# Leading weight tiles of a diffusion backbone: the first norm split into scale, rstd and shift

## The chip, the cores and the metric

One core of a Trainium2 chip runs the whole program. The metric is the device time of one execution in microseconds (us), the median of several runs. TensorE is called PE, VectorE DVE, ScalarE ACT, GpSimd POOL, and SyncE SP; SP here only issues transfers.

## The reference

Two layers over 256 latent tokens and 256 context tokens, 1024 wide, float32. Each layer is half a SwiGLU feed-forward, a token mixer (latent attention in layer 0, windowed attention in layer 1), and another half feed-forward. Before each of the six sub-layers stands a norm with adaLN. What the change touches is the first of them, in layer 0:

```python
mx = split(silu(c) @ mod_w[0] + mod_b[0], 9)       # shift, scale, gate, ...; the same for c_ctx
h  = rms_norm(x, g) * (1 + scale) + shift
x  = x + 0.5 * gate * ((silu(h @ w_gate) * (h @ w_up)) @ w_out)
```

In the kernel's words: x stands transposed, 8 tiles of 128 features by 512 tokens (both streams side by side). With G = g (1 + scale) per feature and r = rstd per token, h = x G r + shift, and a product with a weight tile W is W·h.

## The kernel before, in words

Float32 products are made of three passes: each operand is split into a high and a low half (the cast on ACT, line 198, the difference on DVE, line 199), and `mm3` multiplies high by high, high by low and low by high (lines 226, 227, 228). A weight tile of 128 outputs has 8 k-blocks, so 24 such matmuls of 512 columns; 44 tiles make the gate and up halves of a feed-forward. Split weights lie in rings of four (`whi`, `wlo`), raw weights in a ring of three, PE's results in eight banks.

The opening of the program, before the first feed-forward, is what the change rewrites. SP issues the loads in program order: the four loads of x (512 KB each), then for each k the four pieces of adaLN column k (shift and scale, two halves of the contraction each, 256 KB), with the four leading weight tiles (512 KB, into the `big` ring) behind columns 0, 1, 3 and 5. Eight transfers are in flight at a time: a load waits for the eighth before it. ACT loads four small constants on its own queue.

`fill(40)` keeps PE busy with multiplies of ones that nobody reads (line 88). ACT squares x (line 964), DVE adds the squares, PE sums them over the features and turns the root's inverse back over the tokens (lines 972 to 989): r is in SBUF before the first product. For each k, `mod_sums` multiplies the columns by silu(c) (16 small matmuls, line 143), ACT copies the sums, PE transposes them (line 151), DVE adds bias and halves and makes the gain (lines 158 to 160). `inputs(k)` makes h of tile k: DVE x G r (line 999), ACT adds the shift and casts (line 1001), DVE takes the low half (line 1002). `lead_products` then multiplies tile k with as many of the four leading weight tiles as are split. All four are held in banks until `ffn` asks for them.

The order on each engine is a static list that a scheduler writes when the program is built: an engine works its list from front to back and waits at an instruction whose operands are missing. `behind(ins)` pins a place in it.

From the third f on `ffn` calls `pump`, which advances the adaLN of later sub-layers in the background: DVE multiplies and adds columns (lines 169 and 171), PE sums them (line 177). For each f, ACT takes silu of the gate bank (line 426), DVE multiplies it with the up bank (line 428), and the product is split.

Of the kernel before, what the change touches and what calls it, by code (L numbers as in the profile page):

```python
# [37 lines left out]
def hybrid_backbone_kernel(ctx, tc, t, out):  # L38
# [40 lines left out]
    nc.vector.memset(ones, 1.0)  # L79
# [3 lines left out]
    def fill(n, after=None):  # L83

        b = bank()
        with behind(after):
            for _ in range(n):
                nc.tensor.matmul(b[:, :P], lhsT=ones, rhs=ones, start=True, stop=True)

    def behind(ins):  # L90

        return tc.issue_after(ins.ins) if ins else nullcontext()
# [33 lines left out]
            elif c in (2, 8):  # L126
                nc.vector.tensor_scalar_mul(v, v, 0.5)

    def load_column(k):

        raws = [[], []]
        for i in range(2):
            for c in range(2):
                raw = r2k().bitcast(F32)
                nc.sync.dma_start(raw, t["modo"][k, c, i])
                raws[c].append(raw.rearrange("p (k n) -> p k n", k=4))
        return raws

    def mod_sums(raws):
        psA = bank()  # L140
        for kt in range(KT // 2):
            for j in range(4):
                nc.tensor.matmul(psA[32 * j:32 * j + 32, :P], lhsT=cond32[:, j % 2 * 4 + kt, :], rhs=raws[j // 2][j % 2][:, kt],
                                 start=(kt == 0), stop=(kt == KT // 2 - 1), skip_group_check=True)
        return psA

    def mod_on_pe(k, psA, n=0, after=None):
        sA = tmp()[:, :P]
        nc.scalar.copy(sA, psA[:, :P])
        psB = bank()[:, :P]  # L150
        turned = nc.tensor.transpose(psB, sA, ident)
        if n:
            fill(n, turned)
        vB = psB.rearrange("p (c i r) -> p c i r", c=2, i=2)
        v = mod[0][:, :, :2 * KT].rearrange("p s (c k) -> p c s k", c=2)[:, :, :, k]
        bias = modb[:, 0, :2 * KT].rearrange("p (c k) -> p c k", c=2)[:, :, k:k + 1].to_broadcast([P, 2, 2])
        with behind(after):
            nc.vector.tensor_tensor(v, vB[:, :, 0, 0:2], bias, ALU.add)
        nc.vector.tensor_tensor(v, vB[:, :, 1, 0:2], v, ALU.add)
        nc.vector.scalar_tensor_tensor(coefA[0][:, :, 0, k], v[:, 1], 1.0, ng[:, 0, 0, k:k + 1].to_broadcast([P, 2]), ALU.add, ALU.mult)  # L160

    def mod_in_background(l, c, streams):
        acc = [big().bitcast(F32)[:, :1024] for _ in streams]
# [102 lines left out]
    def load_table(func, q):  # L266

        d = small(1)
        nc.scalar.activation(d, q[:, 0:1], func, scale=1.0 if func == AF.Sqrt else -1.0)

    class Sublayer:


        def __init__(self, l, sub, streams, first, leads=None, both=2):
            self.l, self.sub, self.streams, self.first = l, sub, streams, first
            self.leads, self.both = leads or streams, both
            self.squares = {s: Squares(KT) for s in streams}
            self.hs = []
            self.lead, self.r = [], {}
            self.end = None  # L280

        def grown(self, s, d):
            if s in self.streams:
# [128 lines left out]
    def ffn(sl, nxt, per_tile=0, late=0):  # L412
        l, which, streams = sl.l, sl.sub // 2, sl.streams
        w = T * len(streams)
        outs = sl.products(ffn_specs(l, which))
        done = sl.end
        for g, (f0, f1) in enumerate(GROUPS):
            gu = []
            for f in range(f0, f1):
                n = 0 if f < late else per_tile + (6 * late <= f < 8 * late)  # L420
                pump(n // 2, done)
                og = next(outs)
                pump(n - n // 2, done)
                ou = next(outs)
                sg = tmp()
                nc.scalar.activation(sg[:, :w], og[:, :w], AF.Silu)  # L426
                pr = tmp()
                nc.vector.tensor_tensor(pr[:, :w], ou[:, :w], sg[:, :w], ALU.mult)  # L428
# [529 lines left out]
        return s  # L958

    sl = Sublayer(0, 0, (0, 1), ffn_specs(0, 0)[:4])  # L960
    squares = None
    for d in range(KT):
        q = tmp()
        nc.scalar.activation(q, xs[d], AF.Square)
        if squares is None:
            squares = q
        else:
            nc.vector.tensor_tensor(squares, squares, q, ALU.add)
    load_table(AF.Sqrt, q)
    total = bank()  # L970
    for j in range(4):
        nc.tensor.matmul(total[:, j:j + 1], lhsT=squares[:, j * P:(j + 1) * P], rhs=ones[:, 0:1], start=True, stop=True)
    raws, wraws = [], []
    for k in range(KT):
        raws.append(load_column(k))
        if k in (0, 1, 3, 5):
            ap, n = sl.first[len(wraws)]
            wraws.append(weight_raw(ap, n, big().bitcast(F32)))

    sums0 = mod_sums(raws[0])  # L980
    root = small()
    nc.scalar.activation(root, total[:, 0:4], AF.Sqrt, scale=1.0 / D, bias=eps)
    nc.vector.reciprocal(root, root)
    wide = bank()
    for j in range(4):
        nc.tensor.transpose(wide[:, j * P:(j + 1) * P], root[:, j:j + 1].to_broadcast([P, P]), ident)
    rstds = [strip() for _ in range(2)]
    for r, cols in zip(rstds, SL):
        nc.scalar.copy(r, wide[:, cols])
    def lead_weight(after=None):  # L990
        with behind(after):
            wt = weight_split(wraws[len(sl.lead)])
        sl.lead.append((wt, bank(), P))

    lead_weight()
    def inputs(k):
        for s in range(2):
            y = strip()
            nc.vector.scalar_tensor_tensor(y, xs[k][:, SL[s]], sl.gain(s, k), rstds[s], ALU.mult, ALU.mult)
            hi, lo = sl.place(s, k)  # L1000
            sl.hi = nc.scalar.activation(hi, y, AF.Identity, bias=sl.shift(s, k))
            sl.end = nc.vector.scalar_tensor_tensor(lo, y, sl.shift(s, k), hi.bitcast(F32), ALU.add, ALU.subtract)

    done = [0] * 4

    def lead_products(n, k1):

        for k in range(k1):
            for i in range(n):
                if done[i] <= k:  # L1010
                    wt, o, M = sl.lead[i]
                    mm3(o, sl.terms(wt, M, slice(0, TT)), (k,), KT)
        done[:n] = [k1] * n

    mod_on_pe(0, sums0, 3)
    inputs(0)
    for k in range(1, KT + 1):
        if k < KT:
            mod_on_pe(k, mod_sums(raws[k]), 5 if k == 1 else 0, sl.end if k == 1 else None)
        lead_products(len(sl.lead), k)  # L1020
        if k < KT:
            inputs(k)
        if k in (1, 3, 5):
            lead_weight(sl.hi)
    qng = load_const("qng", (P, 4))
    kvng = load_const("kvng", (P, 2))
    ropeC = load_const("ropeC", (P, T))
# [117 lines left out]
```

## Time and profile before

| | |
|---|---|
| median of 3 runs | 1699.57 us (1696.93 to 1700.79) |
| the profiled execution's own time | 1699.09 us |
| its span, first to last instruction | 1697.3 us |
| mean granted PE clock | 0.999 |
| PE busy | 1672.6 us, 99% |
| DVE busy | 1080.8 us, 64% |
| ACT busy | 645.4 us, 38% |
| DMA | 243.75 MB, mean 144 GB/s |

A timeline row reads: start, duration, engine, line, operation, output<-inputs, shapes, count, and in brackets the idle time just before and what ended it. An fp32 matmul of two plain fp32 operands shows as two records, so x32 of line 143 are 16 matmuls. Matmuls overlap: a row of 0.39 us may start 0.23 us after the one before. A row of the windows view reads: stretch, its length, then busy time and count for PE, PEld, DVE, ACT and POOL, then granted clock, DMA share and GB/s; where one engine is asked for, its column alone. A row of the waits view reads: who waited for whom, us in total, times, longest. A row of groups reads: count, busy us, mean ns, idle before; a tile's row has the shortest, median and longest duration in ns and the first and last start.

### The profile page before, as it was taken

The page shows a single profiled execution, that of the slowest core. Times are in us where ns is not written, and L with a number is a line of the kernel's source. Part 1 is how long each engine was busy: PE and PEld are TensorE (multiplying, and loading weights), DVE is VectorE, ACT ScalarE, POOL GpSimd, SP SyncE. Part 2 cuts the span into 40 slices and gives each one's busy share as a digit, 9 for nine tenths or more (in the row PEclk, how much of TensorE's full clock was granted, in tenths as well). Part 3 has the DMA queues.
Part 4 walks back from the last instruction along what each step waited for, and adds up shares of the span by engine and source line. Part 5 has one row for each costly group of instructions (what it writes and reads, how often), then busy time and mean ns, then how long its engine had stood idle before and what let it go on. Part 6 is the DMA issues. An engine that isn't in the chain of part 4 may idle for free.

```text
span 1697.3 us, 23433 instructions
## 1 busy us (share of the span) xinstructions
PE 1672.6 (99%) x9294; PEld 1417.5 (84%) x9294; DVE 1080.8 (64%) x1538; ACT 645.4 (38%) x1132; POOL 222.5 (13%) x186
## 2 busy tenths in 40 slices
PE   9999999999999999999999999999999999999997
PEld 7888878888788898788888897888888898789997
DVE  6776777645668568856847365644433367778886
ACT  4421322235556353222222353222222366654444
POOL 0000000004132130000000130000000253133332
PEclk9999999999999999999999999999999999999999
DMA  9655556531211126644645335735332222155553
GB/s 345 220 164 183 167 186 194 162 124 57 88 50 63 56 84 200 207 149 154 208 144 172 107 112 196 234 123 162 114 100 92 95 88 77 62 161 175 174 186 113
DMA packets 71536, 243.75 MB, mean 144 GB/s; under 512 B 8577, under 2 KB 9345, under 8 KB 71425
## 3 DMA queue, kind: packets, MB, share of 16 engines
q1 hardware_dynamic: 70560, 241.54, 43.7%
q8 instruction: 73, 1.20, 0.3%
q10 hardware_dynamic: 864, 0.70, 0.1%
q14 instruction: 39, 0.31, 0.1%
HBM read 241.16 MB, written 1.05 MB: 143 GB/s over the span
## 4 chain that ended last, share of the span: by engine, by line
PE 79%; DMA 5%; DVE 5%; ACT 4%; POOL 3%; issue 2%; ACTq 0%; DVEq 0%; SPq 0%; POOLq 0%
PE bank L226 25%; PE bank L227 25%; PE bank L228 24%; DMA wraw<-in_woutn 4%; POOL wraw L912 3%; DVE wlo L199 2%; ACT whi L198 2%; DMA r2k<-in_modo 1%; PE bank L177 1%; DVE big L171 1%; PE bank L239 1%; DVE small L454 0%; PE bank L482 0%; PE bank L906 0%; DMA modraw<-in_modw 0%
## 5 line engine op out<-in xcount | busy, mean ns | idle before, releaser
L226 PE MATMUL bank<-r2k,whi 128*128 128x512 f32 (+2 forms) x2434 | 866.7, 357 | 0.9 <-ACT small L918 0.9
L227 PE MATMUL bank<-r2k,whi 128*128 128x512 f32 (+2 forms) x2434 | 861.9, 354 | 2.6 <-DVE r2k L202 1.2
L228 PE MATMUL bank<-r2k,wlo 128*128 128x512 f32 (+2 forms) x2434 | 861.4, 354 | 1.1 <-DVE wlo L199 0.9
L198 ACT CAST whi<-wraw 128x1024 fp32r<-128x1024 f32 (+1 forms) x311 | 319.9, 1033 | 851.1 <-PE bank L227 502.1
L226 PEld LDWEIGHTS bank<-r2k,whi 128*128 128x128 f32 x2434 | 459.1, 189 | 79.5 <-ACT whi L198 9.2
L227 PEld LDWEIGHTS bank<-r2k,whi 128*128 128x128 f32 x2434 | 460.2, 189 | 68.4 <-DVE r2k L202 1.9
L228 PEld LDWEIGHTS bank<-r2k,wlo 128*128 128x128 f32 x2434 | 460.1, 189 | 65.8 <-DVE wlo L199 2.0
L199 DVE TENSOR_TENSOR wlo<-wraw,whi 128x1024 fp32r<-128x1024 f32 (+1 forms) x300 | 363.5, 1218 | 117.2 <-ACT whi L198 110.1
L171 DVE SCALAR_TENSOR_TENSOR big<-modraw,conds,big 128x1024 f32<-128x1024 f32 x189 | 233.3, 1278 | 14.7 <-DMA modraw<-in_modw 14.4
L264 POOL TENSOR_TENSOR strip<-strip 128x256 f32<-128x256 f32 x58 | 57.3, 1002 | 939.5 <-ACT strip L258 465.2
L366 DVE SCALAR_TENSOR_TENSOR x<-bank,mod,x 128x256 f32<-128x256 f32 x168 | 74.3, 478 | 154.0 <-PE bank L228 154.0
L428 DVE TENSOR_TENSOR tmp<-bank,tmp 128x512 f32<-128x512 f32 x66 | 45.6, 690 | 160.7 <-PE bank L228 158.1
L912 POOL TENSOR_TENSOR wraw<-wraw,gate 128x1024 f32<-128x1024 f32 x22 | 63.5, 2888 | 127.2 <-DMA wraw<-in_woutn 127.0
L906 PE MATMUL bank<-whi,r2k 128*128 128x512 f32 x176 | 58.0, 392 | 3.1 <-DVE r2k L927 1.8
L927 DVE TENSOR_TENSOR r2k<-tmp,r2k 128x256 fp32r<-128x256 f32 x22 | 51.0, 2318 | 0.9 <-ACT r2k L926 0.9
L199 DVE TENSOR_TENSOR r2k<-bank,r2k 128x512 fp32r<-128x512 f32 (+2 forms) x73 | 40.7, 593 | 16.1 <-ACT r2k L198 15.6
L199 DVE TENSOR_TENSOR r2k<-tmp,r2k 128x512 fp32r<-128x512 f32 x66 | 45.1, 684 | 1.4 <-ACT r2k L198 1.4
L198 ACT CAST r2k<-tmp 128x512 fp32r<-128x512 f32 x66 | 41.0, 622 | 12.8 <-DVE tmp L428 12.4
L454 DVE TENSOR_REDUCE small<-bank 128x1 f32<-128x512 f32 (+1 forms) x64 | 37.0, 614 | 7.4 <-PE bank L777 7.2
L906 PEld LDWEIGHTS bank<-whi,r2k 128*128 128x128 f32 x176 | 33.0, 188 | 10.2 <-DVE r2k L927 2.2
L426 ACT ACTIVATE tmp<-bank 128x512 f32<-128x512 f32 x66 | 38.9, 590 | 3.7 <-PE bank L228 3.7
L198 ACT CAST r2k<-bank 128x512 fp32r<-128x512 f32 (+2 forms) x73 | 34.4, 524 | 12.7 <-PE bank L228 8.8
(195 smaller groups left out, 1147.5 us busy)
## 6 DMA issues: line engine op xcount, KB each, us to landing
wraw<-in_win SPq DMA_DIRECT2D x172, 512.0 KB, 3.9
modraw<-in_modw SPq DMA_DIRECT2D x128, 512.0 KB, 4.2
wraw<-in_wout SPq DMA_DIRECT2D x48, 448.0 KB, 3.3
wraw<-in_wout SPq DMA_DIRECT2D x24, 512.0 KB, 4.4
wraw<-in_woutn SPq DMA_DIRECT2D x22, 512.0 KB, 3.5
r2k<-in_modo SPq DMA_DIRECT2D x32, 256.0 KB, 6.0
wraw<-in_mwo SPq DMA_DIRECT2D x8, 512.0 KB, 3.5
wraw<-in_swq SPq DMA_DIRECT2D x8, 512.0 KB, 3.5
```

The costliest lines, as they stand in the source:

```text
L171: nc.vector.scalar_tensor_tensor(acc[s], raw, conds[:, kt, s:s + 1], acc[s], ALU.mult, ALU.add)
L198: nc.scalar.copy(hi, src)
L199: return engine.tensor_tensor(lo, src, hi.bitcast(F32), ALU.subtract)
L226: nc.tensor.matmul(o, lhsT=ah, rhs=bh, start=(i == 0), stop=False)
L227: nc.tensor.matmul(o, lhsT=ah, rhs=bl, start=False, stop=False)
L228: nc.tensor.matmul(o, lhsT=al, rhs=bh, start=False, stop=(i == n - 1))
L264: nc.gpsimd.tensor_tensor(self.parts[0], self.parts[0], q, ALU.add)
L366: nc.vector.scalar_tensor_tensor(xs[d][:, SL[s]], o[:, SL[s]], mod[l][:, s, c:c + 1], xs[d][:, SL[s]], ALU.mult, ALU.add)
L428: nc.vector.tensor_tensor(pr[:, :w], ou[:, :w], sg[:, :w], ALU.mult)
L906: nc.tensor.matmul(acc[i][h], lhsT=gu[a][:, rows], rhs=w[b][:, cols], start=(f == 0 and j == 0), stop=(f == NF - 1 and j == 2))
L912: nc.gpsimd.tensor_tensor(raw, raw, gate, ALU.mult)
L927: nc.vector.tensor_tensor(gu[1], u, gu[0].bitcast(F32), ALU.subtract)
```

## The change

W·h is written as r (W·(G x)) + W·shift for the four leading tiles. They multiply z = G x, split into high (ACT, line 1028 of the new file) and low (DVE, line 1029), without r and without the shift. r and the shift join when the banks are read: for the first two f, DVE multiplies the gate and up banks by r, ACT adds the gate's W·shift in the silu, DVE adds the other and multiplies. W·shift comes from 32 small matmuls (line 1110) and a transpose (line 1115), with a table of the shifts in `gate`, a tile that is loaded later on.

The loads are reordered: x 0 and 1, the scale columns of 0 and 1 (four pieces), two weight tiles; then x, the scale columns of two features, and a weight tile, twice; then x 6 and 7 with their scale columns; then all shift columns two features at a time, and two more weight tiles through the `wraw` ring. `mod_sums` now treats two scale or two shift columns in one go, and a product with `both_halves` (line 161) adds the two halves of the contraction where a transpose stood. Squares are taken between the gained tiles, and r after the last of them. The full h is still made (`inputs`, lines 1048 to 1051), for the two further tiles and all others. Twelve fills stand around the first scale sums and twelve around the second.

```diff
-    for d in range(0, KT, 2):
+    def load_x(d):
         nc.sync.dma_start(x_all[:, d:d + 2], t["xT"][:, d:d + 2])
+    load_x(0)
...
+    def mod_sums(raws, n=0):
         psA = bank()
...
         sA = tmp()[:, :P]
         nc.scalar.copy(sA, psA[:, :P])
+        if n:
+            fill(n)
+        v = bank()[:, :4]
+        turned = nc.tensor.matmul(v, lhsT=sA, rhs=both_halves.rearrange("p a s -> p (a s)"), start=True, stop=True)
         if n:
             fill(n, turned)
...
+                if sl.ends is not None and f < 2:
+                    nc.vector.tensor_tensor(sg, og, sl.rstds, ALU.mult)
+                    nc.vector.tensor_tensor(pr, ou, sl.rstds, ALU.mult)
+                    for s in streams:
+                        nc.scalar.activation(sg[:, SL[s]], sg[:, SL[s]], AF.Silu, bias=sl.ends[:, 2 * f, s:s + 1])
+                        nc.vector.scalar_tensor_tensor(pr[:, SL[s]], pr[:, SL[s]], sl.ends[:, 2 * f + 1, s:s + 1], sg[:, SL[s]],
+                                                       ALU.add, ALU.mult)
...
+    scales.append(load_columns(0, 1))
+    load_weight()
+    load_weight()
+    for k in range(2, KT, 2):
+        load_x(k)
+        scales.append(load_columns(k, 1))
+        if k < 6:
+            load_weight()
+    for k in range(0, KT, 2):
+        shifts.append(load_columns(k, 0))
+        if k in (2, 4):
+            more.append(weight_raw(*ffn_specs(0, 0)[len(more) + 4]))
...
+    def gained(d):
+        z = (r2k(), r2k())
+        for s in range(2):
+            nc.scalar.activation(z[0][:, SL[s]], xs[d][:, SL[s]], AF.Identity, scale=sl.gain(s, d))
+            sl.end = nc.vector.scalar_tensor_tensor(z[1][:, SL[s]], xs[d][:, SL[s]], sl.gain(s, d), z[0][:, SL[s]].bitcast(F32),
+                                                    ALU.mult, ALU.subtract)
+        zs.append(z)
...
+    v = mod_sums(scales[0], 6)
+    lead_weight()
+    mod_scale(0, v)
+    gained(0)
+    gained(1)
+    lead_products(1, 1)
+    lead_weight()
+    squares(0)
+    for k in range(2, KT, 2):
+        lead_products(1, k)
+        v = mod_sums(scales[k // 2], 6 if k == 2 else 0)
+        lead_products(len(sl.lead), k)
+        mod_scale(k, v)
+        gained(k)
+        gained(k + 1)
+        if k < 6:
+            lead_weight()
+        q = squares(k)
...
+    lead_products(4, KT - 2)
+    rstds = rstds_of_x()
+    for k in range(0, KT, 2):
+        v = mod_sums(shifts[k // 2])
+        if k == 0:
+            lead_products(4, KT - 1)
+        mod_shift(k, v)
+        inputs(k)
+        inputs(k + 1)
+        if k in (2, 4):
+            more[k // 2 - 1] = (weight_split(more[k // 2 - 1]), bank(), P)
+    lead_products(4, KT)
+    def products_of_inputs():
+        for k in range(KT):
+            for wt, o, M in more:
+                mm3(o, sl.terms(wt, M, slice(0, TT)), (k,), KT)
...
+        for k in range(KT):
+            for j in range(4):
+                nc.tensor.matmul(b[32 * j:32 * j + 32, :P], lhsT=shift32[:, k], rhs=wraws[j][:, k * P:(k + 1) * P],
+                                 start=(k == 0), stop=(k == KT - 1), skip_group_check=True)
```

How the lists of the engines move, at three places. ACT before, from the start to the first operand of a product (`L1001`; `big` holds a raw leading weight tile, `r2k` the operand):

```order
L97 ACTIVATE conds<-c_cond 128x16
L964 ACTIVATE tmp<-x 128x512 x8
L269 ACT_TABLE_LOAD
L269 ACTIVATE small<-tmp 128x1
L982 ACTIVATE small<-bank,eps 128x4
L149 COPY tmp<-bank 128x128
L989 COPY strip<-bank 128x256 x2
L198 CAST whi<-big 128x1024
L149 COPY tmp<-bank 128x128
L1001 ACTIVATE r2k<-strip,mod_127 128x256 x4
```

ACT in the change, to the same point (`L1028`):

```order
L100 ACTIVATE conds<-c_cond 128x16
L216 CAST whi<-big 128x1024 x2
L157 COPY tmp<-bank 128x128
L1012 ACTIVATE tmp<-x 128x512 x2
L216 CAST whi<-big 128x1024 x2
L1028 ACTIVATE r2k<-x,coefA_126 128x256 x4
L157 COPY tmp<-bank 128x128
```

One weight cast stood before the first operand; now all four leading tiles are cast before it, and two of the eight squares remain there.

PE before, from the first fills behind column sums on:

```order
L88 MATMUL bank<-ones 128x128 x3
L143 MATMUL bank<-r2k,cond_124 32x128 x16
L151 MATMUL bank<-c_ident,tmp 128x128
L88 MATMUL bank<-ones 128x128 x5
L226 MATMUL bank<-r2k,whi 128x512
L227 MATMUL bank<-r2k,whi 128x512
L228 MATMUL bank<-r2k,wlo 128x512
L143 MATMUL bank<-r2k,cond_124 32x128 x16
```

PE in the change, from the first product on:

```order
L244 MATMUL bank<-r2k,whi 128x512
L245 MATMUL bank<-r2k,whi 128x512
L246 MATMUL bank<-r2k,wlo 128x512
L244 MATMUL bank<-r2k,whi 128x512
L245 MATMUL bank<-r2k,whi 128x512
L246 MATMUL bank<-r2k,wlo 128x512
L154 MATMUL bank<-r2k,cond_121 32x128 x16
L91 MATMUL bank<-ones 128x128 x6
L161 MATMUL bank<-both_halves,tmp 128x4
L91 MATMUL bank<-ones 128x128 x6
```

Before, no fill stood behind the first product; now twelve do, and the second group of sums, which stood ahead of all products, stands behind six of them.

The last place is the end of the opening, where the last two shift columns are summed. ACT in the change:

```order
L157 COPY tmp<-bank 128x128
L216 CAST whi<-wraw 128x1024 x2
L1050 ACTIVATE r2k<-strip,mod_124 128x256 x2
L157 COPY tmp<-bank 128x128
L1050 ACTIVATE r2k<-strip,mod_124 128x256 x2
```

and PE between its last two products with `both_halves`, and what follows:

```order
L161 MATMUL bank<-both_halves,tmp 128x4
L154 MATMUL bank<-r2k,cond_121 32x128 x16
L245 MATMUL bank<-r2k,whi 128x512
L246 MATMUL bank<-r2k,wlo 128x512
L161 MATMUL bank<-both_halves,tmp 128x4
L244 MATMUL bank<-r2k,whi 128x512
```

The copy that the second `L161` needs now stands behind two casts of further weight tiles. From the seventh weight tile on the lists of PE are alike but for line numbers.

More of the change, by code (lines that the diff above doesn't have):

```diff
@@ L974, in hybrid_backbone_kernel @@
[L974 to L996, printed above, removed]
-        for s in range(2):
[L998 to L1002, printed above, removed]
+    wraws, scales, shifts, more = [], [], [], []
@@ L1010, in lead_products @@
                 if done[i] <= k:
[L1011 to L1019, printed above, removed]
[L1020 to L1024 removed]
+                    (wh, wl), o, M = sl.lead[i]
@@ new lines, in lead_products, with inputs @@
+                    cols = slice(k * P, (k + 1) * P)
+                    mm3(o, {k: ((wh[:, cols], wl[:, cols]), zs[k])}, (k,), KT)
+        done[:n] = [max(k1, n) for n in done[:n]]
+    def inputs(k):
+        for s in range(2):
+            y = strip()
+            nc.vector.scalar_tensor_tensor(y, xs[k][:, SL[s]], sl.gain(s, k), rstds[:, SL[s]], ALU.mult, ALU.mult)
+            hi, lo = sl.place(s, k)
+            sl.hi = nc.scalar.activation(hi, y, AF.Identity, bias=sl.shift(s, k))
+            sl.end = nc.vector.scalar_tensor_tensor(lo, y, sl.shift(s, k), hi.bitcast(F32), ALU.add, ALU.subtract)
@@ new lines, in rstds_of_x @@
+    def rstds_of_x():
+        for j in range(4):
+            nc.tensor.matmul(total[:, j:j + 1], lhsT=totals[0][:, j * P:(j + 1) * P], rhs=ones[:, 0:1], start=True, stop=True)
+        root = small()
+        nc.scalar.activation(root, total[:, 0:4], AF.Sqrt, scale=1.0 / D, bias=eps)
+        nc.vector.reciprocal(root, root)
+        wide = bank()
+        for j in range(4):
+            nc.tensor.transpose(wide[:, j * P:(j + 1) * P], root[:, j:j + 1].to_broadcast([P, P]), ident)
+        r = r2k().bitcast(F32)
+        nc.scalar.copy(r, wide)
+        return r
```

95 lines of the change are left out of this document (63 added, 32 removed).

## The prediction

> **What bounds the kernel now.** The page first: how busy TensorE (PE) is over the whole span, and what it waits for.
>
> ```profile
> span 1697.3 us, 23433 instructions
> ...
> PE 1672.6 (99%) x9294; PEld 1417.5 (84%) x9294; DVE 1080.8 (64%) x1538; ACT 645.4 (38%) x1132; POOL 222.5 (13%) x186
> ```
>
> Then PE's own waits over the whole span, longest first, of which these are the first, the third and the sixth:
>
> ```profile
> PE bank L803 <- ACT r2k L795: 2.5, 1, 2.5
> ...
> PE bank L906 <- DVE r2k L927: 1.8, 1, 1.8
> ...
> PE bank L143 <- DMA r2k<-in_modo: 1.1, 4, 0.4
> ```
>
> No wait later in the program is longer than 2.5 us, so a microsecond that the opening loses or gains passes to the end nearly whole. Busy is no measure of use there: in the first 40 us PE runs throw-away multiplies (L88) and slow column sums. So I count the opening as a ledger: the time at which PE has finished a known amount of weight products, less that amount at its steady pace. The timeline gives the rows; they are not neighbours.
>
> ```profile
> 1.03 11.58 PE L88 MATMUL bank<-ones 128*128 128x128 f32 x80 [1.03 <-DVE ones L79]
> ...
> 18.06 1.28 PE L88 MATMUL bank<-ones 128*128 128x128 f32 x10
> ...
> 19.10 0.48 PE L226 MATMUL bank<-r2k,whi 128*128 128x512 f32 x1
> ...
> 45.10 1.08 PE L143 MATMUL bank<-r2k,cond 128*32 128x128 f32 x32
> 46.11 0.50 PE L226 MATMUL bank<-r2k,whi 128*128 128x512 f32 x1
> ...
> 53.06 0.40 PE L227 MATMUL bank<-r2k,whi 128*128 128x512 f32 x1
> ...
> 61.92 0.39 PE L227 MATMUL bank<-r2k,whi 128*128 128x512 f32 x1
> ...
> 95.79 1.06 PE L177 MATMUL bank<-big,ones 128*32 128x512 f32 x8
> ```
>
> From 53.06 to 61.92 there are 39 steps (13 triples of lines L226 to L228): 0.227 us each. L177 is a good post: in both programs 12 whole weight tiles of 24 products, 288, stand before it on PE. They cost 288 x 0.227 = 65.4 us, so 95.79 - 65.4 = **30.4 us** went to other things: 19.1 until the first product, and 11.3 after it, of which six groups of column sums at 46.11 - 45.10 = 1.01 are 6.1. In that opening the DMA is the other limit:
>
> ```profile
> 0.00:10.00 10.00, 8.97 (x59) 8.97 (x60) 3.75 (x10) 5.82 (x10) 0.19 (x4) 1.00 0.84 301
> 10.00:20.00 10.00, 9.38 (x122) 8.06 (x120) 6.07 (x16) 4.86 (x11) 0.00 (x0) 1.00 1.01 372
> 20.00:30.00 10.00, 9.13 (x118) 6.26 (x118) 7.41 (x20) 5.29 (x11) 0.00 (x0) 1.00 1.05 392
> ```
>
> The last number is GB/s. The queues are full until 30 us.
>
> **The change part by part. First: when the first product can start.** It needs the scale columns of 0 and 1 and x 0 and 1, which are now early. But the order on ACT, shown above, decides otherwise: the four activations L1028 that make the first operand stand behind the casts of all four leading weight tiles, the fourth included, and that tile is the nineteenth transfer of the SP queue. When does it land? In bytes ahead of it and its own: three x loads and four weight tiles of 512 KB, twelve column pieces of 256 KB, 6656 KB. In the kernel before, column 2 ended the same count at 6144 KB (four x loads, two tiles, twelve pieces), and the last of it was waited for until 21.50:
>
> ```profile
> 21.50 1.06 PE L143 MATMUL bank<-r2k,cond 128*32 128x128 f32 x26 [0.27 <-DMA r2k<-in_modo]
> ...
> r2k<-in_modo SPq DMA_DIRECT2D x32, 256.0 KB, 6.0
> ...
> big<-in_win SPq DMA_DIRECT2D x4, 512.0 KB, 6.0
> ```
>
> 512 KB more is 0.524 MB / 392 GB/s = 1.3 us: 22.8. Lower bound: by 20.0 us 3.01 + 3.72 = 6.73 MB had moved in all, and 6656 KB are 6.82 MB, so not before 20.2 at these rates; upper bound some 23.5. I take 22.8, from the row nearest to it. Then one cast and two halves of the operand:
>
> ```profile
> 15.56 1.06 ACT L198 CAST whi<-big 128x1024 fp32r<-128x1024 f32 x1
> ...
> 16.66 1.23 DVE L199 TENSOR_TENSOR wlo<-big,whi 128x1024 fp32r<-128x1024 f32 x1
> ...
> 17.74 0.91 ACT L1001 ACTIVATE r2k<-strip,mod 128x256 fp32r<-128x256 f32 x2
> ...
> 20.73 0.88 DVE L1002 SCALAR_TENSOR_TENSOR r2k<-strip,mod,r2k 128x256 fp32r<-128x256 f32 x2 [0.18 <-ACT r2k L1001]
> ```
>
> 22.8 + 1.06 + 0.91 and 0.1 for the hand-over: first product at **24.9**, against 19.10. What waits behind that cast is everything: ACT's L1028, DVE's L1029, all of PE.
>
> **Second: PE work that is no product, after that start.** Seven groups of column sums instead of six (a group now holds two scale or two shift columns, so eight groups remain, but only one is ahead of the start): 7 x 1.01 = 7.1. Twelve throw-away multiplies stand between the second group and the products; five took 1.28 (18.06, two records each), 0.25 each: 3.0. The row sums of squares and their turning, hidden before the first product until now, stand in the middle of the products:
>
> ```profile
> 12.45 0.95 PE L972 MATMUL bank<-ones,tmp 128*128 128x1 f32 x8
> ...
> 14.34 0.65 PE L986 MATMUL bank<-c_ident,small 128*128 128x128 f32 x4
> ...
> L151 PE MATMUL bank<-c_ident,tmp 128*128 128x128 f32 x8 | 2.3, 285 | 0.4 <-ACT tmp L149 0.4
> ```
>
> 0.95 + 0.65 = 1.6. Seven products with both_halves (L161) take the place of transposes; they are of the kind of L972, 0.24 each, at least half of that if pipelined: 7 x 0.2 = 1.4. New are 32 small products of the shift (L1110), of the shape of L143's 16: 2.0, and one transpose, 0.1. Sum 7.1 + 3.0 + 1.6 + 1.4 + 2.1 = 15.2. The other side of this work is a multiply by rstd and an add that leave L999 to L1002; those are DVE and ACT work, and no PE time comes back for them. Six instead of four tiles before the steady part is only the order of the same 288.
>
> **Third: waits.** On DVE the low half of the fourth tile (1.23) stands before the first L1029 (0.88), while PE has one product of 0.23 to do: 1.2 with the second operand's share. Five round trips over ACT's copy at 0.1: 0.5. At the last shift columns ACT does two casts and two activations, 2 x 1.06 + 0.91, before the copy that PE needs (the rows above); PE has one group and two products, 1.5, to fill it: 2.0 with the copy of 0.27 and hand-overs. DVE then: eight operations instead of two for the first two f, and the sums of the background chunk before L177:
>
> ```profile
> L171 DVE SCALAR_TENSOR_TENSOR big<-modraw,conds,big x14: 1274/1279/1282, 58.9 to 91.3; 128x1024 f32<-128x1024 f32 x14
> ...
> L169 DVE TENSOR_SCALAR big<-modraw,conds x2: 745/746/746, 57.5 to 58.2; 128x1024 f32<-128x1024 f32 x2
> ...
> L428 DVE TENSOR_TENSOR tmp<-bank,tmp 128x512 f32<-128x512 f32 x66 | 45.6, 690 | 160.7 <-PE bank L228 158.1
> ...
> 52.00:95.00 43.00, 43.00 (x190) 35.40 (x189) 36.50 (x37) 17.23 (x24) 0.00 (x0) 1.00 0.67 217
> ```
>
> Now they end at 91.3 + 1.3 = 92.6, 3.2 ahead of PE: this cover is what the change uses up. Its chunk stands on DVE behind the f 0 and 1. From the end of the first six tiles PE has 2.1 of L1110 and 144 products, 34.8 us, until L195. DVE has in that stretch the chunk (2 x 0.746 + 14 x 1.279 = 19.4), five low halves of weights (6.2), four multiplies by rstd and four adds of half width (4 x 0.69 + 4 x 0.44 = 4.5), and three multiplies and five low halves of results (8 x 0.69 = 5.5): 35.6, and it begins some 0.4 later. 1.2 late, bounds 0 and 2.5. Last, the pace after standing still:
>
> ```profile
> 1.00:6.00 5.00, 4.97 (x23) 1.00 0.85 286
> 6.00:12.60 6.60, 6.60 (x62) 1.00 1.04 386
> ```
>
> These are the throw-away multiplies: 4.6 records per us until 6, 9.4 after, though the granted clock reads 1.00. PE started from rest at half pace for 5 us. In the change PE rests from about 17 to 24.9. If that repeats, 2.5 us go, of which the first operands' waits hide about half: I take 1.2, bounds 0 and 2.5. The Trainium skill, "TensorE: Matmul & The Clock Gate", Part 1, states the rule: the array's clock is halved after an idle window of about 3.4 us and comes back after as much sustained work; by it the sum keeps this term, without it the total is 1.2 us lower. The trace agrees for the start (4.6 against 9.4 records per us); it shows no later rest of that length.
>
> Waits: 1.2 + 0.5 + 2.0 + 1.2 + 1.2 = 6.1. **Sum:** 24.9 + 15.2 + 6.1 = 46.2, against 30.4: 15.8 us more. The profiled execution took 1699.1 (span 1697.3), the median is 1699.57: 1699.1 + 15.8 = **1714.9**.
>
> **Edits that I cost at nothing.** The shift columns land late but 4 x 24 products of 0.227 (21.8 us) cover them from 24.9 on: the last piece ends 13312 KB of loads, 7.34 MB past column 2's 6144 KB, so it lands near 21.5 + 7.34 / 0.392 = 40.2, when by my sums less than half of these 96 products are done. Without that cover each pair of columns, 1024 KB, is 2.7 us. The load of gate now waits for L1110; the weight loads behind it wait for their own buffers as long.
>
> **Rivals.**
> (a) The fourth tile is not what decides: it lands as early as the operands could use it. Then the fills end at 12.6 (1.03 + 11.58), one group 1.0, copy, L161 and the scale about 1, the operand 0.9: first product at 15.5. The last scale piece, 8192 KB in, lands at 21.5 + 2.10 / 0.392 = 26.9, early enough behind 72 products. With 15.2 and 3 of the waits (0.5, 2.0, 0.5): 33.7, so 1702.4. For it: no byte of the first operand is missing. Against it: the byte count, 20.2 at the least.
> (b) Faster: halving the column bytes ahead of the products starts PE early and keeps it fed. With no wait at all after the start the ledger is T + 15.2, and it beats 30.4 only for a first product before 15.2; a gain of 0.2% (3.4 us) needs 11.8, and the fills alone hold PE until 12.6. With (a)'s start of 15.5 and all 3.0 of fills inside gaps: 27.7, 1696.4; the groups too would have to fall into gaps for more. For it: the first operand needs half the column bytes. Against it: ACT's order, and 9 us of new or uncovered PE work.
> (c) The loss is given back: a later stage waits now for data that comes at its own time, so that the delay drains away, 1699. Against it: the list of PE's waits has no such entry above 2.5 us.
> (d) DVE becomes the bound in the first feed-forward and holds PE at each chunk: 3 us more, 1718. For it: 36.50 busy of 43; against it: it recovers 3.2 per chunk now.
>
> **How the numbers follow.** Forecast 0.80; (a) 0.08; (b) 0.04; (c) 0.03; (d) 0.05. The forecast's own range: 2.6 off for the earliest landing, 1.2 each for DVE and pace, 1 for fills that run inside a wait, not all together: 1710; upward 1.3 each for DVE and pace, 0.7 for the landing and 1 for buffer waits not counted: 1719. The range 1706 to 1719 leaves out (a), (b), (c) and a little of (d), under 2 in 10. 0.2%, 3.4 us, is about what a measurement of this kernel can tell from no change. Faster: (b), 0.04. Same: (c) and (a) where it stays under 1703, 0.08. Slower: the rest, 0.88.
>
> **What would show it.** First product L244 near 24.9, with the fourth whi cast near 22.8 just before L1028 on ACT; PE idle or at rest from 17 to there; L195 at about 111.6 instead of 95.79, after the same 288 products; no DMA wait on shift columns; the rest of the program shifted as a whole. A first product before 20, or an L195 before 100, would prove me wrong; a later stage shorter than before, too.

## The result, and the profile after

The changed kernel takes **1714.46 us** (median of 4 runs, 1711.34 to 1716.31) against 1698.25 before (4 runs beside it, 1696.7 to 1700.79): ratio **1.009**, 95% interval 1.0072 to 1.0109, slower. Its profiled execution took 1714.77 us, its span is 1713.0.

The page's first rows of the changed kernel:

```profile
span 1713.0 us, 23677 instructions
...
PE 1679.0 (98%) x9399; PEld 1423.9 (83%) x9399; DVE 1082.0 (63%) x1553; ACT 652.5 (38%) x1150; POOL 219.5 (13%) x186
```

PE is busy 6.4 us more, and the span is 15.7 us longer; the other 9.3 are idle time. PE's waits, longest first:

```profile
PE bank L244 <- ACT r2k L1028: 9.7, 1, 9.7
PE bank L830 <- ACT r2k L822: 2.5, 1, 2.5
PE bank L933 <- DVE r2k L954: 1.8, 1, 1.8
```

The second and third are the two longest single waits of the kernel before, unchanged. The first is new: PE stands for 9.7 us ahead of its first product. The timeline over that time, of ACT and of the DVE operation that finishes the first gain:

```profile
16.17 0.17 DVE L174 TENSOR_TENSOR coefA<-coefA,ng 128x4 f32<-128x4 f32 x1
...
18.67 1.04 ACT L216 CAST whi<-big 128x1024 fp32r<-128x1024 f32 x1 [3.34 <-DMA big<-in_win]
...
23.95 1.04 ACT L216 CAST whi<-big 128x1024 fp32r<-128x1024 f32 x1 [4.24 <-DMA big<-in_win]
24.90 1.70 ACT L1028 ACTIVATE r2k<-x,coefA 128x256 fp32r<-128x256 f32 x4
```

The gain is there at 16.34. ACT waits 3.34 us for the third weight tile and 4.24 for the fourth, and only then makes the first operand. Now PE's timeline: the first products, the first two groups of column sums after them, and L195, the post behind the same 288 weight products:

```profile
25.86 0.80 PE L244 MATMUL bank<-r2k,whi 128*128 128x512 f32 x1 [9.69 <-ACT r2k L1028]
27.10 0.79 PE L245 MATMUL bank<-r2k,whi 128*128 128x512 f32 x1 [0.45 <-DVE r2k L1029]
...
29.53 1.94 PE L154 MATMUL bank<-r2k,cond 128*32 128x128 f32 x32
...
37.41 1.08 PE L154 MATMUL bank<-r2k,cond 128*32 128x128 f32 x32
...
65.72 0.38 PE L161 MATMUL bank<-both_halves,tmp 128*128 128x4 f32 x2 [0.79 <-ACT tmp L157]
...
111.93 1.06 PE L195 MATMUL bank<-big,ones 128*32 128x512 f32 x8
```

The post stood at 95.79 and stands at 111.93, 16.1 later; the span is 15.7 longer. The group of sums at 29.53 takes 1.94, the one at 37.41 1.08. The windows view of PE (its busy time, then granted clock, DMA share, GB/s) shows why:

```profile
20.00:21.00 1.00, 0.00 (x0) 1.00 1.03 403
21.00:22.00 1.00, 0.00 (x0) 0.75 1.04 408
22.00:23.00 1.00, 0.00 (x0) 0.50 1.01 391
...
30.00:31.00 1.00, 1.00 (x24) 0.50 1.03 383
31.00:32.00 1.00, 1.00 (x16) 0.63 1.04 373
32.00:33.00 1.00, 1.00 (x12) 1.00 1.02 336
```

During the wait the granted clock falls to 0.50, and it is whole again only near 31.7 (the mean of 0.63 from 31 to 32 puts the step there), 5.9 us after the first product.

### The profile page after: what moved, and what is told of

It is laid out like the page before. It is cut to its first block, busy times and chain, and to the rows that moved or that the text cites. A ratio compares the mean times of both kernels' runs of the same rounds, so it can differ in the third digit from the quotient of the medians.

```text
span 1713.0 us, 23677 instructions
## 1 busy us (share of the span) xinstructions
PE 1679.0 (98%) x9399; PEld 1423.9 (83%) x9399; DVE 1082.0 (63%) x1553; ACT 652.5 (38%) x1150; POOL 219.5 (13%) x186
## 4 chain that ended last, share of the span: by engine, by line
PE 79%; DMA 6%; DVE 5%; ACT 4%; POOL 3%; issue 2%; ACTq 0%; SPq 0%; DVEq 0%; POOLq 0%
PE bank L244 25%; PE bank L245 24%; PE bank L246 24%; DMA wraw<-in_woutn 4%; POOL wraw L939 3%; DVE wlo L217 2%; ACT whi L216 2%; PE bank L195 1%; DMA modraw<-in_modw 1%; DVE small L481 0%; PE bank L509 0%; PE bank L257 0%; PE bank L933 0%; DMA r2k<-in_modo 0%; DVE big L189 0%
## 5 line engine op out<-in xcount | busy, mean ns | idle before, releaser
L217 DVE TENSOR_TENSOR r2k<-bank,r2k 128x512 fp32r<-128x512 f32 (+2 forms) x73 | 40.7, 593 | 16.1 <-ACT r2k L216 15.6
L954 DVE TENSOR_TENSOR r2k<-tmp,r2k 128x256 fp32r<-128x256 f32 x22 | 46.6, 2120 | 0.9 <-ACT r2k L953 0.9
```

The source lines that it names most:

```text
L217: return engine.tensor_tensor(lo, src, hi.bitcast(F32), ALU.subtract)
L954: nc.vector.tensor_tensor(gu[1], u, gu[0].bitcast(F32), ALU.subtract)
```

## The experiments

**One yardstick.** Between the first product and the post, each PE row's step (from its start to the next row's start, its idle time apart) is put to its line; of products only what goes beyond 0.227 us each counts. This table is worked out in that way from the timelines. It sums to the ledger, and each kernel has 288 products in it:

| us | before | after | e3 | e1 | e2 | e4 | e7 |
|---|---|---|---|---|---|---|---|
| first product | 19.10 | 25.86 | 25.82 | 16.39 | 16.95 | 13.59 | 17.70 |
| column sums | 7.58 | 7.93 | 7.07 | 7.07 | 7.79 | 8.88 | 7.21 |
| fills | 0 | 2.92 | 2.78 | 2.78 | 0 | 0 | 0 |
| turning the sums (L151, L161) | 0.14 | 1.34 | 1.35 | 1.33 | 1.38 | 1.36 | 0.64 |
| sums of squares and their turning | 0 | 1.35 | 1.35 | 1.36 | 1.35 | 1.36 | 1.37 |
| the shift's product (L1110, L1115) | 0 | 1.91 | 1.92 | 1.91 | 1.91 | 1.92 | 1.91 |
| idle | 0.88 | 1.24 | 1.53 | 0.79 | 1.18 | 2.28 | 0.85 |
| products beyond 0.227 | 2.71 | 4.00 | 2.70 | 2.72 | 3.16 | 3.54 | 2.79 |
| **ledger** | **30.4** | **46.5** | **44.5** | **34.3** | **33.7** | **32.9** | **32.5** |

**e1_pin: is it the fourth tile's cast?**

```diff
+    first = (sl.hi, sl.end)
...
-            lead_weight()
+            lead_weight(first if k == 2 else (sl.hi, sl.end))
```

`sl.hi` and `sl.end` are the last operations of an operand on ACT and DVE; `lead_weight(after)` pins the cast and the low half behind them; `first` is taken behind the operands of 0 and 1.

> The change with one thing altered: the casts of the third and fourth leading weight tile are pinned on ACT and DVE behind the operands they stood in front of. My theory (ACT's list holds the first operand until the fourth tile lands): first product near 17.4 us instead of 25.9, PE never rests long enough for its clock to fall, background sums L195 near 101 us instead of 111.9, time 1703 to 1705. Rival (the DMA is the limit in the opening, so an earlier start only waits later for scale columns): the start moves but L195 stays above 108, time 1710 or more. Second rival (the start is worth its 8.5 us but the clock's 2 us stay): L195 near 103, 1706.

Measured: 1704.76 us (6 runs, 1703.96 to 1706.69) beside 1699.51, ratio 1.0032 (1.0021 to 1.0044). ACT and PE in its timeline:

```profile
15.43 1.71 ACT L1029 ACTIVATE r2k<-x,coefA 128x256 fp32r<-128x256 f32 x4 [1.03 <-DVE coefA L174]
17.88 1.05 ACT L216 CAST whi<-big 128x1024 fp32r<-128x1024 f32 x1 [0.74 <-DMA big<-in_win]
...
16.39 0.50 PE L244 MATMUL bank<-r2k,whi 128*128 128x512 f32 x1 [0.56 <-ACT r2k L1029]
...
99.73 1.06 PE L195 MATMUL bank<-big,ones 128*32 128x512 f32 x8
```

The operand is made before the third tile is even there, the first product comes 9.5 us earlier and the post 12.2, at 99.73 where some 101 was expected. PE's list is the same in both. At the post, three quarters of the loss were the place of two casts on ACT, with their low halves on DVE; between the medians it is 9.7 of 16.2 us. The loads and their order are unchanged, so these 12.2 were no limit of the DMA alone.

**e3_keepwarm: what is the fallen clock worth?**

```diff
+    fill(36)
```

These are throw-away multiplies between the first column sums and the first product.

> The change with 36 more throw-away multiplies between the first scale sums and the first product, so that PE doesn't rest from 16.2 to 25.9; order otherwise alike. My theory (the clock falls to half in the rest and makes the next products and sums slow): granted clock 1.0 throughout, first product unchanged at 25.9, L195 2 us earlier, near 109.9, time about 1712.4. Rival (the slow stretch is hidden behind the waits for the operands' low halves and the second scale sums): L195 within 0.5 us of 111.9, same time.

```profile
25.82 0.50 PE L244 MATMUL bank<-r2k,whi 128*128 128x512 f32 x1 [0.61 <-ACT r2k L1028]
...
109.90 1.06 PE L195 MATMUL bank<-big,ones 128*32 128x512 f32 x8
```

The first product starts at the same time as in the changed kernel, and takes 0.50 in place of 0.80; the granted clock reads 1.00 from 10 us to the post, and the post is 2.0 us earlier. That is the price of the fallen clock. The median, 1714.7 (4 runs, 1712.97 to 1720.27; ratio 1.0095, 1.008 to 1.011), does not resolve 2 us; the ledger does.

**e2_pin_nofill: what do the twelve fills cost?**

```diff
-        v = mod_sums(scales[k // 2], 6 if k == 2 else 0)
+        v = mod_sums(scales[k // 2])
```

> The same with the twelve throw-away multiplies around the second scale sums taken out as well. My theory (they stand in the way of products): 3 us less than with the pins alone, L195 near 98, time 1700 to 1702. Rival (they run in gaps in which PE would wait for the second operands anyway): L195 within 0.5 us of the pins alone, same time.

1702.23 us (10 runs, 1701.16 to 1703.84), ratio 1.0018 (1.0008 to 1.0027). A miss at the post: 3.0 earlier than e1 expected, 0.63 measured. Between the medians of e1 and e2 it is 2.5.

```profile
16.95 0.51 PE L244 MATMUL bank<-r2k,whi 128*128 128x512 f32 x1 [0.28 <-ACT r2k L1029]
...
20.40 0.38 PE L161 MATMUL bank<-both_halves,tmp 128*128 128x4 f32 x2 [0.39 <-ACT tmp L157]
...
22.21 0.62 PE L154 MATMUL bank<-r2k,cond 128*32 128x128 f32 x10
22.76 0.50 PE L244 MATMUL bank<-r2k,whi 128*128 128x512 f32 x1
23.19 0.84 PE L154 MATMUL bank<-r2k,cond 128*32 128x128 f32 x18
...
99.10 1.06 PE L195 MATMUL bank<-big,ones 128*32 128x512 f32 x8
```

Two things ate the gain. A wait of 0.39 for ACT's copy now stands where a fill ran. And the scheduler wrote another list: the third group of sums is cut by products into pieces, which costs 0.72 in the sums and 0.44 in the products that restart behind them. The start is 0.56 later too, but that is within what two profiles of one list differ by (see e7). So the fills did take 2.8 us of PE, and a version without them pays 1.6 of it back: 1.2 us are gained behind the first product.

**e4_best: is a still earlier start worth its time?**

```diff
-    fill(40)
+    fill(24)
...
-        if n:
-            fill(n)
...
+        with behind(sl.hi), behind(sl.end):
+            q = squares(k)
```

The two removed lines are the fills ahead of the first product with `both_halves`; the fills at the second sums are left out as in e2. All four casts, and the squares, now stand behind operands, and DVE makes the table of the conditions ahead of the norm's table.

> The change's idea carried through as well as the order allows: 24 instead of 40 fills at the start, the table of the conditions ready before the norm's table, no fills in the way of the first and second sums, each weight cast and each square pinned behind the operands. My theory (what remains is 12 to 14 us of PE work that is no product and had been hidden, and the DMA's supply of scale columns): first product near 13, L195 at 94.5 to 96.5, time 1697.5 to 1700, no gain that can be told from none. Rival (the idea of the change is sound and only its order was bad): L195 at 91 or less, time below 1694.5.

1703.21 us (11 runs, 1700.46 to 1705.71), ratio 1.002 (1.0011 to 1.0029): not below e2, and a miss (1697.5 to 1700 expected, the post at 94.5 to 96.5).

```profile
13.59 0.50 PE L243 MATMUL bank<-r2k,whi 128*128 128x512 f32 x1 [0.89 <-ACT whi L215]
...
17.04 1.06 PE L155 MATMUL bank<-r2k,cond 128*32 128x128 f32 x26 [0.33 <-DMA r2k<-in_modo]
...
22.34 0.41 PE L155 MATMUL bank<-r2k,cond 128*32 128x128 f32 x4 [0.27 <-DMA r2k<-in_modo]
...
30.71 1.08 PE L155 MATMUL bank<-r2k,cond 128*32 128x128 f32 x32
```

The post is at 98.31. The start is 3.36 earlier than in e2, and what follows takes 2.57 more: 1.1 of idle time, 1.1 of sums in pieces (the row at 22.34 is a piece of 4 records) and 0.4 of products that restart behind them. The second and third groups of sums wait for scale columns: from 17.04 to 22.34 two x tiles, two scale columns and a weight tile arrive, 2048 KB in 5.3 us, 396 GB/s. Where e2 has its fourth group at 31.53, e4 has it at 30.71. That the supply sets this stage is argued, not shown: PE's waits for the DMA in it come to 0.6 us, and the pieces are the order that the scheduler chose.

**e5_turn and e6_noshift: is the rest PE work?**

```diff
-        v = bank()[:, :4]
-        turned = nc.tensor.matmul(v, lhsT=sA, rhs=both_halves.rearrange("p a s -> p (a s)"), start=True, stop=True)
+        psB = bank()[:, :P]
+        turned = nc.tensor.transpose(psB, sA, ident)
...
+        v = ring.tile([P, 2, 2], F32, tag="pair", name="pair", bufs=2)
+        nc.vector.tensor_copy(v, vB[:, :, 1, 0:2])
+        nc.vector.tensor_tensor(v, vB[:, :, 0, 0:2], v, ALU.add)
```

This is e5, against e2. e6 is e5 without the 32 small matmuls of the shift's product, so its first two f lack W·shift.

> This is the version with pinned weight casts and without the fills at the second sums (post L195 at 99.10, 1702.23), where the product with both_halves (L161) is turned back into what stood there before the change, a transpose by the identity, and DVE adds the two halves of the contraction in two small operations. My theory: what is left of the loss is PE work after the first product, and every piece of it counts. In that version the seven L161 take 1.38 us of PE's steps; the transposes L151 of the kernel before take 0.02 each, 0.14 in all. So the post comes 1.2 earlier, 97.9, less what the two DVE operations (0.17 each) put in front of the first operand, up to 0.4: 97.9 to 98.3, and the time falls to about 1701.1. The rival: in this stage PE waits for scale columns anyway, so the L161 stand in gaps; then the post stays at 99.1 or comes later by the DVE operations, 99.1 to 99.5, and the time at 1702.2.

> The version with transposes, and the shift's product with the four leading weight tiles is left out (32 small matmuls L1110, one transpose L1115, their copy and their table; the ends are zero, so the first two f lack W times shift). My theory: these matmuls stand in the middle of products whose operands are ready, at 1.91 us of PE's steps, so the post comes 1.9 earlier than in the version with transposes: about 96.0 to 96.4, the ledger at 30.6 to 31.0 against 30.4 before the change, and the time at about 1699.2, no longer to be told from the kernel before. The rival: DVE or ACT hold the products there (banks that come free late, background sums on DVE), and the matmuls only fill a wait; then the post moves by less than 0.7 and the time stays above 1700.5.

Both missed the time by more than 20 us: e5 1726.07 (4 runs, 1724.73 to 1727.74; ratio 1.0157, 1.0142 to 1.0173), e6 1723.99 (4 runs, 1721.45 to 1724.27; ratio 1.014, 1.0123 to 1.0157). Each post came at least half a microsecond later than expected (98.91 for 97.9 to 98.3, 96.88 for 96.0 to 96.4), but between the two it moved as expected:

```profile
98.91 1.06 PE L199 MATMUL bank<-big,ones 128*32 128x512 f32 x8
```

```profile
96.88 1.06 PE L199 MATMUL bank<-big,ones 128*32 128x512 f32 x8
```

(e5, then e6): 2.0 us for the shift's product. But no wait of PE had grown by 2 us, and nothing in the opening accounts for the 22 us by which the span of e5 is longer than that of e2. The groups view of e2, then of e5, in the line that holds a third of all products:

```profile
L244 PE MATMUL bank<-r2k,whi 128*128 128x512 f32 (+2 forms) x2434 | 866.4, 357 | 1.2 <-ACT small L945 0.9 <-ACT r2k L1029 0.3
```

```profile
L248 PE MATMUL bank<-r2k,whi 128*128 128x512 f32 (+2 forms) x2434 | 873.3, 360 | 1.9 <-ACT r2k L1033 1.2 <-ACT small L949 0.3 <-ACT r2k L220 0.2
```

The mean record is 3 ns longer: products had become slower over the whole program. Two explanations stood: the transposes and DVE operations, or the new ring of two 32-byte tiles, which had pushed the split weights 64 bytes further in SBUF while the operands r2k stayed.

**e7 to e12: the edit or the place?** e7, e8, e9, e11 and e12 are e5 with the sums in an existing ring; they differ in an unused tile ahead of the split weights. e10 is e2 with such a tile of 64 bytes and nothing else. The distances below are counted from the kernel's buffer sizes in the order of their rings; no view of the profile shows an address.

```diff
+    gap = ring.tile([P, 16], F32, tag="gap", name="gap", bufs=1)
+    nc.gpsimd.memset(gap, 0.0)
```

> The version with transposes again, but the two features' sums lie in an existing ring of small tiles, and an unused tile of 256 bytes stands ahead of the split weights: from the first operand buffer r2k to the first weight buffer whi there are 138240 bytes per partition, 135 KB, where it was 134 KB (137216) in the change and 117 KB (119808) in the kernel before. In the first version with transposes a new ring of two 32-byte tiles had made it 137280, 64 bytes off the whole KB, and the products' pitch was 0.233 in place of 0.227. Theory one, the place in SBUF sets the pitch: here it is back at 0.227, the post L195 comes at 97.0 to 97.9 (98.91 less 288 x 0.0067 = 1.9) and the time is about 1700.5. Theory two, the edit itself (transposes or the two DVE operations) slows PE for the whole program: the pitch stays at 0.233, the post at 98.9 and the time at 1726.

> The same without the unused tile: the distance from r2k to whi is 137984, a whole number of KB plus 768. If any distance that is not a whole KB costs, the pitch is 0.233 and the time 1723 to 1726. If only a distance that is off a multiple of 128 or 256 bytes costs, the pitch is 0.227 and the time 1700.5. If it is the edit and not the place, 1726 here and in the version at 135 KB.

> The same with an unused tile of 768 bytes: the distance is 138752, a whole number of KB plus 512. If the distance has to be a whole KB, the pitch is 0.233 and the time 1723 to 1726; if half a KB or less is enough, 0.227 and 1700.5.

> The version with pinned casts and without the fills at the second sums (post 99.10, 1702.23), word for word, but for an unused tile of 64 bytes ahead of the split weights, set once by POOL. No engine's work changes beside that one write. If the place of the weights alone sets the pitch, it is 0.233 here, the post comes 1.9 later at 101.0 and the time is 1724 to 1727. If it was the transposes, the pitch stays at 0.227, the post at 99.1 and the time at 1702.2.

> The version with transposes and small tiles, with an unused tile that makes the distance from r2k to whi a whole number of KB plus 128. Distances of 0, 512 and 768 past a whole KB gave a pitch of 0.227, 64 gave 0.233. If the distance has to be a multiple of 256, the pitch is 0.233 and the time 1724 to 1727; if a multiple of 128 is enough, 0.227 and 1700 to 1702.

> The same with the distance a whole number of KB plus 32. If every distance that is off the grid costs the same, the pitch is 0.233 and the time 1724 to 1727; if only an odd multiple of 64 costs (both operands on a grid of 64 but in different halves of 128), it is 0.227 and 1700 to 1702. A pitch below 0.227 would be a faster layout than that of any version so far.

| | bytes from r2k to whi | past a whole KB | pitch, us | time, us | ratio |
|---|---|---|---|---|---|
| before | 119808 | 0 | 0.2269 | 1699.13 | |
| after | 137216 | 0 | 0.2269 | 1714.46 | 1.009 (1.0072 to 1.0109) |
| e2 | 137216 | 0 | 0.2269 | 1702.23 | 1.0018 (1.0008 to 1.0027) |
| e10 | 137280 | 64 | 0.2333 | 1728.29 | 1.0173 (1.0156 to 1.019) |
| e7 | 138240 | 0 | 0.2269 | 1700.96 | 1.0013 (1.0004 to 1.0022) |
| e8 | 137984 | 768 | 0.2269 | 1702.02 | 1.0014 (1.0005 to 1.0024) |
| e9 | 138752 | 512 | 0.2269 | 1701.42 | 1.0014 (1.0005 to 1.0023) |
| e11 | 138368 | 128 | 0.2323 | 1728.39 | 1.0173 (1.0143 to 1.0203) |
| e12 | 138272 | 32 | 0.2333 | 1729.27 | 1.0178 (1.0149 to 1.0208) |

The pitch is the mean step from one product to the next, read from the longest stretch of products alone behind the post, 214 steps in each; each ratio is against runs of the kernel before beside it, and the medians of e11 and e12 are of two runs. The first and last rows of that stretch in e2, and in e10:

```profile
106.35 0.40 PE L245 MATMUL bank<-r2k,whi 128*128 128x512 f32 x1
...
154.90 0.39 PE L246 MATMUL bank<-r2k,wlo 128*128 128x512 f32 x1
```

```profile
107.67 0.39 PE L245 MATMUL bank<-r2k,whi 128*128 128x512 f32 x1
...
157.60 0.40 PE L246 MATMUL bank<-r2k,wlo 128*128 128x512 f32 x1
```

48.55 us in the one, 49.93 in the other, with a granted clock of 1.00 in both. One write on POOL is all that e10 adds, and the lists of PE are the same, so the place sets the pitch; that the transposes or DVE set it is ruled out. Distances of 0, 512 and 768 past a KB run at the better pitch, 32, 64 and 128 at the worse, as if the distance had to be a multiple of 256 bytes. This does not explain the change itself: it moved both buffers, but its distance is a whole number of KB as before, and its pitch is the same.

With the place mended, the question of e5 has its answer in e7:

```profile
17.70 0.50 PE L248 MATMUL bank<-r2k,whi 128*128 128x512 f32 x1 [0.78 <-ACT r2k L1033]
...
97.85 1.06 PE L199 MATMUL bank<-big,ones 128*32 128x512 f32 x8
```

Turning the sums costs 0.64 in place of 1.38. Behind its first product e7 gains 2.0 us on e2: 0.74 in the turning, 0.58 in the column sums, and the rest in idle time and joints. The post is at 97.85, 96.90 and 97.23 in e7, e8 and e9 (whose lists for PE are the same), 97.3 in the mean against 99.10. The spread of the three, 0.95 between profiles of one list, comes nearly all from the first product (16.57 to 17.70). So the small differences above, 0.63 of e1 and e2 and 0.8 of e2 and e4, are not settled by one profile each; the time from the first product to the post repeats within 0.2. The shift's product was not taken out again at the better place.

No version here beats the kernel before. The nearest, e7, stands 0.13% above it. Behind the first product it still pays 1.4 for the sums of squares and 1.9 for the shift's product, which did not stand there before, and its earlier start gives 1.4 back.

## Why the prediction was right, point by point

**The first product, 24.9; measured 25.86.** The mechanism was the predicted one: all of ACT's first operands behind the fourth cast, shown by e1. The step that failed by a size is the landing: 22.8 was taken, scaled in bytes from column 2's landing, and the cast's row above has 23.95, 1.15 later and 0.45 past the upper bound named (23.5). Cast, operand and hand-over took 1.9, the predicted 2. The scaling took the rates of the kernel before, 301 and 372 GB/s in the first two stretches of 10 us. With the loads in their new order the changed kernel has (PE's busy time, then granted clock, DMA share, GB/s)

```profile
0.00:10.00 10.00, 8.97 (x66) 1.00 0.83 265
10.00:20.00 10.00, 6.17 (x75) 1.00 1.00 377
```

By 20 us that is 0.31 MB less, 0.8 us at 392 GB/s, and most of the 1.15. Why the first stretch moves fewer bytes stays open.

**Work that is no product, 15.2; measured 14.5 at full pace** (e3's column sums 7.07, fills 2.78, L161 1.35, rstd 1.35, shift 1.92). Each term is within 0.3 of its own. Only, the fills' 3.0 is a price in place, and not all of it a gain to be had: without them e2 got back 0.6 at the post, 1.2 behind the first product and 2.5 between the medians. Of the 11.3 in the kernel before, the column sums took 7.58 and not the 6.1 that the prediction read; the forecast does not rest on that.

**Waits, 6.1; this sum came out near by luck, for wrong reasons.** The half pace after the rest was taken at 1.2 and is 2.0 (e3). The wait for the fourth tile's low half was taken at 1.2, and its idle time is 0.45 (27.10 above). The wait at the last shift columns was taken at 2.0 and is 0.79 (65.72 above): ACT's casts begin 0.5 ahead of the group that PE has to fill the time, and not with it.

```profile
62.72 1.99 ACT L216 CAST whi<-wraw 128x1024 fp32r<-128x1024 f32 x2
...
63.19 1.08 PE L154 MATMUL bank<-r2k,cond 128*32 128x128 f32 x32
```

DVE was to be 1.2 late at L195 and is not late: no idle time stands ahead of the post. All idle time on PE from the first product to the post is 1.24. What the sum left out are the joints: a product behind other work starts its successor some 0.32 us later, not 0.227, one ahead of other work is late too, and all of it is 2.7 us, in the kernel before as well. There they were inside the measured 11.3, but the new sum was built from parts, and had no line for them. The parts behind the first product add to 21.3 against 20.7 measured, and the start was 1.0 short; so 46.2 met 46.5, and 1714.9 met 1714.46, because the errors cancel.

**The ledger's rule, that a microsecond of the opening passes to the end.** It held for the change (16.1 at the post, 15.7 in the span) and for e2, e3, e8 and e9 within 1 us; for e1 and e4, 3.9 and 2.5 at the post became 5.2 and 4.6 in the span, and for e7 2.1 became 0.2. Short stretches of half clock late in the program go with this. The profile of e1 has two of some 3.4 us (PE's busy time, then granted clock, DMA share, GB/s):

```profile
1465.00:1468.00 3.00, 3.00 (x15) 0.51 0.00 0
1680.00:1683.00 3.00, 2.88 (x13) 0.52 0.53 168
```

So has that of e4; the kernel before, the change, e2, e8 and e9 have one ahead of the last microseconds, e7 none. That they make the difference is not shown (e3 has none either, and its 14.1 at the post became 13.9). The recorded runs point the same way: those of e7 took 1698.2 to 1700.3 us at a mean granted clock of 0.999 and 1701.4 to 1702.5 at 0.997. The rule failed for e5, e6, e10, e11 and e12, because the pace behind the post had changed. The rule needs the products' pitch checked beside it.

**The rivals.** (a) asked that the fourth tile not decide. It did; e1, which makes it not decide, starts at 16.39 where (a) said 15.5 and takes 1704.8 where (a) said 1702.4. (b), faster, found no support even in a version with an early start: e4 starts at 13.59, and its ledger is 32.9, because 2.57 of the 3.36 us are lost again behind the start. (c): from the post to the end the change takes 0.4 us less than the kernel before, so next to nothing is given back. (d): in the first feed-forward DVE is busy 39.57 of 43 us, and PE does not wait for it:

```profile
70.00:113.00 43.00, 43.00 (x250) 34.50 (x248) 39.57 (x50) 17.95 (x27) 0.00 (x0) 1.00 0.63 200
```

The shift columns, costed at nothing, made no DMA wait on PE. Part of their cover was the delay itself; but in e1, with products from 16.39 on, no group of shift sums waits for a column either.

## What to carry to other kernels

On an engine that works its list in order, look at what stands ahead of the operand that everything waits for: a cast of a tile that is needed later, but is listed first, costs its tile's landing time, and moving two of them was worth 12 us at the post here, where the edit's new matmuls together were worth some 4.5 (1.2 for turning, 1.35, 1.9). When an edit adds or drops a tile, check the pitch of the main loop before reading anything else: a shift of 64 bytes in SBUF cost 1.5% of this program (e10 against e2), more than the change under study. A loss built up from parts wants a line for the joints between them.

## What the runs showed of the hardware

**The place of the weights.** Matmuls of 512 columns go from 0.2269 us to 0.2333 (2.8%) when the distance per partition between the moving operand's buffers and the weights' is 32 or 64 bytes past a whole KB, and to 0.2323 at 128. Five versions have the slower pitch (e5 and e6, too, at 64), and every version at 0, 512 or 768 the faster; 256 itself was not tried. Why is open: which of the two reads is held up was not tried, nor whether it is the distance that counts or the weights' address alone, since r2k lay at one place in all versions from the change on.

**The clock.** In the changed kernel PE's last work ahead of the wait ends at about 16.2. The granted clock stays at 1.00 until 21, has a mean of 0.75 from 21 to 22, and is 0.50 from then on, so it fell near 21.5, 5.3 us after that work. It came back near 31.7, 5.9 us after the first product. By the Trainium skill, "TensorE: Matmul & The Clock Gate", Part 1, activity is watched in free-running windows of about 3.4 us. By an estimate from that figure a rest is seen after one to two windows, 3.4 to 6.8 us. Both delays here lie in it. The price of this rest was 2.0 us (e3 against the change); the prediction had bounds of 0 and 2.5 for it.
